# The inverses of the even mixer without zero padding: 64x64 products, two banks side by side, masks and copies on 128 partitions

## The chip, the cores and the metric

The kernel runs on one core of a Trainium2 chip. The time is device microseconds of one execution; given are the median of three runs and their range. A shorter time is better.

## The reference, cut to what matters

The program is a decoder trunk of two residual layers on 512 tokens of width 1024, in float32. The first (even) layer has an RWKV-7 mixer with 8 heads of 64 channels beside a pooling mixer, the second attention beside a state-space layer; each is followed by a layer of 32 routed experts. The change lies in the RWKV-7 recurrence alone:

```python
def step(state, inp):
    r_t, w_t, k_t, v_t, a_t, b_t = inp
    sa = jnp.einsum('bhij,bhj->bhi', state, a_t)
    state = (state * w_t[:, :, None, :] + sa[..., None] * b_t[:, :, None, :]
             + v_t[..., None] * k_t[:, :, None, :])
    return state, jnp.einsum('bhij,bhj->bhi', state, r_t)
```

The other parts of a layer are `x += Mixer(RMSNorm(x))` and `x += HierMoE(RMSNorm(x))`.

## The kernel before, in words

The recurrence is not stepped token by token. The 512 tokens are cut into 8 chunks of 64. Inside a chunk the part with `a` and `b` is a unit lower triangular 64x64 matrix, and its inverse turns the chunk into a few products; from chunk to chunk only a 64x64 state is handed on. Two heads share the 128 partitions (64 channels each), so there are four pairs of heads, `c` = 0 to 3.

For each pair the code has generators, which hand control back after every few instructions. `prep(c)` makes scaled keys and queries: `XX[H[h], h, 0]` and `[..., 1]` for head h, and `bk`, which holds `bt` and `kt`. `H` is the lower and the upper half of the partitions. `invert(c)` makes the inverses of the 8 chunks. `chain(c)` first joins them to maps (`maps`: products `pdx`, copied to `DX`, then `pgy`, added to `XX`) and then steps through the chunks (`steps`: products `pS` and `py`). `finish(c)` normalizes the result and gates it. One call of `run_all` interleaves `chain` and `finish` of one pair with `invert` of the next and `prep` of the one after it, and with products `po` of the output projection.

`invert` starts with products of `bt`, `kt` and `XX`: `pab` (the matrix transposed, and a part of the output), `paa` (the matrix, and a part of the input) and `prk`. VectorE copies them out of PSUM through constant masks (L455, L457, L469, L473, L482), and POOL adds the unit matrix (L456, L470) or applies one more mask (L474). Then five levels double the size of the inverted diagonal blocks, b = 2, 4, 8, 16, 32. A level has two halves, of four chunks each. In a half, products of `AT` and `D` go to a bank `pg`; VectorE masks them to `Gp` (L498); products of `Gp` and `DT` go to a bank `pd`, in two terms (L505, L510); VectorE copies one term to `D` (L512) and ScalarE the other to `DT` (L513), or in the last level to `DP` (L516).

All these products are written with operands of 128 rows: the operand of head h in one half of the partitions, and zeros in the other half, so that the other head's rows, which stand in the second operand, add nothing. `AT`, `Gp`, `DP` and `DX` have room for that, `[128, 8, 2, 64]` or the like, and are zeroed once; `XX` is zeroed for each pair (L379, POOL). Since head h lands in 64 of the 128 PSUM partitions, a product is one of 128 rows by 64 columns of the array, and the two heads lie beside each other. What is padded is masked and copied in two instructions of 64 partitions each, one for each head. In the profile a float32 product of PE shows as two records.

The banks of `invert` are two PSUM tiles that are taken in turn (`bank`, tag "ps").

The order of the instructions on each engine is not that of the code: the program is built with a scheduler that runs an estimate of the timeline and puts the instructions of each engine in a fixed order, which the engine then follows. Inside that order an engine waits for semaphores. After the even mixer the memory of its tiles is given to the ring of buffers into which SyncE loads the expert weights.

## Time and profile before

| | us |
|---|---|
| median of 3 runs | 1644.34 |
| lowest, highest | 1642.44, 1648.06 |
| the profiled execution | 1643.12 |
| its span, first to last instruction | 1641.4 |
| PE busy in the span | 1528.8 |
| VectorE (DVE) busy | 819.5 |
| ScalarE (ACT) busy | 447.9 |
| GpSimd (POOL) busy | 230.4 |
| HBM read | 452.91 MB |

The mean granted TensorE clock is 0.975 of full speed. The even mixer takes about the first 380 us, its inverses lie between 111 and 334 us. The profile names engines PE (TensorE's products), PEld (its weight loads), DVE, ACT, POOL and SP (SyncE). Busy times of PE are those of overlapping products whose ends are modelled, so a busy PE is not PE at its peak. An instruction is named by its line in the kernel, its operation and its tiles, output first.

### The profile page before, as it was taken

How to read it: one execution, taken by the hardware profiler on the slowest of the kernel's cores; microseconds unless marked ns; L12 is line 12 of the kernel's file. 1: busy time of each engine (PE TensorE's matmuls, PEld its weight loads, DVE VectorE, ACT ScalarE, POOL GpSimd, SP SyncE). 2: the span in 40 equal slices, each digit the busy share in tenths (PEclk: the TensorE clock that was granted, in tenths of full speed). 3: DMA queues.
4: the chain of work that ended last, by engine and by line, in shares of the span. 5: the costliest groups of instructions: out<-in, count | busy, mean ns of one | idle time of the engine just before them, and what ended most of it. 6: DMA issues, size and time to landing. Idle time of an engine off the chain costs nothing. (4 is left out here: it accounts for less than half of the span.)

```text
span 1641.4 us, 24906 instructions
## 1 busy us (share of the span) xinstructions
PE 1528.8 (93%) x9852; PEld 886.1 (54%) x9852; DVE 819.5 (50%) x1942; ACT 447.9 (27%) x1029; POOL 230.4 (14%) x268
## 2 busy tenths in 40 slices
PE   8998988999999999999998998799999999999997
PEld 6776666776444444433348775577544444433433
DVE  5577878776233333332764694764433333322323
ACT  5234434332212121111314533741021211211110
POOL 2342331200000000000211242501000000000000
PEclk9999999999999999999999999799999999999999
DMA  7210100177899999999992262209789999999996
GB/s 223 97 65 21 51 4 2 53 295 294 337 420 419 419 420 420 420 419 418 420 387 63 66 94 59 103 26 356 308 363 420 419 420 420 419 420 421 420 420 236
DMA packets 95564, 453.62 MB, mean 276 GB/s; under 512 B 12507, under 2 KB 30715, under 8 KB 49360
## 3 DMA queue, kind: packets, MB, share of 16 engines
q1 hardware_dynamic: 88144, 438.01, 67.9%
q0 software_dynamic: 5968, 13.58, 2.4%
q8 instruction: 80, 1.31, 0.3%
q10 hardware_dynamic: 1328, 0.36, 0.1%
q14 instruction: 44, 0.36, 0.1%
HBM read 452.91 MB, written 6.78 MB: 280 GB/s over the span
## 5 line engine op out<-in xcount | busy, mean ns | idle before, releaser
L1198 PE MATMUL pgu<-w,XT 128*64 128x512 f32 x1920 | 452.4, 596 | 22.3 <-DMA w<-in_moe_w_gate 19.1
L1198 PEld LDWEIGHTS pgu<-w,XT 128*64 128x64 f32 x1920 | 141.9, 137 | 312.3 <-issue 256.6
L1288 DVE TENSOR_TENSOR x<-pc,x 128x512 f32<-128x512 f32 x240 | 149.3, 682 | 163.6 <-PE pc L1198 163.6
L1198 PE MATMUL pd<-w,hTe 128*64 128x512 f32 x960 | 213.9, 598 | 0.6 <-ACT hTe L1336 0.6
L1327 DVE SCALAR_TENSOR_TENSOR hid<-hid,gs,pgu 128x512 f32<-128x512 f32 x32 | 23.9, 747 | 242.6 <-PE pgu L1198 234.9
L1095 POOL DMA_INDIRECT rows<-rows,idx x30 | 30.0, 999 | 759.6 <-DVE O L1215 590.3
L1198 PEld LDWEIGHTS pd<-w,hTe 128*64 128x64 f32 x960 | 66.6, 137 | 122.7 <-issue 112.9
L1256 ACT ACTIVATE XT<-pga,p_norm 128x128 f32<-128x128 f32 x240 | 68.3, 371 | 195.1 <-PE pga L1198 191.3
L1345 DVE TENSOR_TENSOR ylo<-pd,yhi 128x512 fp32r<-128x512 f32 (+1 forms) x68 | 44.8, 659 | 138.8 <-ACT yhi L1344 138.8
L1326 ACT ACTIVATE hid<-pgu,gs 128x512 f32<-128x512 f32 x32 | 22.0, 688 | 288.9 <-PE pgu L1198 288.9
L1198 PE MATMUL pc<-yhi,S 128*128 128x512 f32 x240 | 100.4, 418 | 0.0
L1198 PE MATMUL pc<-ylo,S 128*128 128x512 f32 x240 | 94.9, 395 | 0.0
L1344 ACT ACTIVATE yhi<-pd 128x512 fp32r<-128x512 f32 (+1 forms) x68 | 38.9, 572 | 170.9 <-PE pd L1198 153.4
L161 DVE SCALAR_TENSOR_TENSOR wlo<-w,p_norm,whi 128x512 fp32r<-128x512 f32 (+1 forms) x72 | 56.3, 813 | 44.9 <-ACT whi L160 44.9
L160 ACT ACTIVATE whi<-w,p_norm 128x512 fp32r<-128x512 f32 (+1 forms) x72 | 46.3, 692 | 77.8 <-PE pu L665 42.3
L1198 PEld LDWEIGHTS pc<-yhi,S 128*128 128x128 f32 x240 | 45.3, 189 | 34.1 <-issue 26.0
L664 PE MATMUL pu<-hhi,whi 128*128 128x512 f32 x144 | 58.6, 411 | 0.2 <-DVE u L672 0.2
L665 PE MATMUL pu<-hlo,whi 128*128 128x512 f32 x144 | 57.8, 401 | 0.0
L1884 PE MATMUL pu<-wlo,hhi 128*128 128x512 f32 x128 | 53.4, 419 | 3.4 <-DVE wlo L161 3.4
L666 PE MATMUL pu<-hhi,wlo 128*128 128x512 f32 x144 | 55.2, 402 | 0.0
L1883 PE MATMUL pu<-whi,hhi 128*128 128x512 f32 x128 | 51.0, 416 | 1.7 <-ACT us L1895 1.7
L1885 PE MATMUL pu<-whi,hlo 128*128 128x512 f32 x128 | 52.5, 416 | 0.0
(539 smaller groups left out, 2502.7 us busy)
## 6 DMA issues: line engine op xcount, KB each, us to landing
w<-in_moe_w_down SPq DMA_DIRECT2D x120, 1024.0 KB, 20.0
w<-in_moe_w_gate SPq DMA_DIRECT2D x120, 1024.0 KB, 20.0
w<-in_moe_w_up SPq DMA_DIRECT2D x120, 1024.0 KB, 20.2
w<-in_even_w_in SPq DMA_DIRECT2D x8, 1024.0 KB, 5.2
w<-in_moe_w_gate SPq DMA_DIRECT2D x16, 512.0 KB, 8.2
w<-in_moe_w_up SPq DMA_DIRECT2D x16, 512.0 KB, 9.6
w<-in_moe_w_down SPq DMA_DIRECT2D x16, 512.0 KB, 9.3
w<-in_odd_w_in SPq DMA_DIRECT2D x8, 1024.0 KB, 5.1
```

The lines of the kernel that those rows point to most:

```text
L160: nc.scalar.activation(hi[:, k, :], w[:, k, :], AF.Copy, scale=g[:, k:k + 1])
L161: nc.vector.scalar_tensor_tensor(lo[:, k, :], w[:, k, :], g[:, k:k + 1], r32(hi[:, k, :]), op0=OP.mult, op1=OP.subtract)
L664: nc.tensor.matmul(out[j], a, hhi[:, kt, :], start=kt == 0, stop=False)
L665: nc.tensor.matmul(out[j], a, hlo[:, kt, :], start=False, stop=False)
L666: nc.tensor.matmul(out[j], b, hhi[:, kt, :], start=False, stop=kt == KD - 1)
L1198: return self.K.tc.keep_in_program_order(op(*args, **kw))
L1256: nc.scalar.activation(self.XTs[j][:, k, :], p[:, i, :], AF.Copy, scale=B.gain[:, k:k + 1])
L1288: V.tensor_tensor(self.x[:, t, c], p, self.x[:, t, c], OP.add)
L1345: self.nc.vector.tensor_tensor(yl[:, c], p, r32(yh[:, c]), OP.subtract)
L1883: nc.tensor.matmul(out[j], a, whi[:, k, :], start=kt == 0, stop=False)
L1884: nc.tensor.matmul(out[j], a, wlo[:, k, :], start=False, stop=False)
L1885: nc.tensor.matmul(out[j], b, whi[:, k, :], start=False, stop=kt == KD - 1)
```

## The change

The zero padding goes, and every product of the inverse, of `pdx` and of `pgy` reads only the 64 partitions in which its head lies. A product then uses 64 rows of the array, lower or upper, and 64 columns, lower or upper (for `pgy` 128). Which head lands in which half of PSUM is chosen for each product: `same` or `other`. Where there are two terms, they are written side by side into two banks, so that one term uses the quarters of the array that the other leaves free.

The new head of `invert`, with the helper that issues the products:

```diff
+        x = lambda z: lambda h: s.XX[H[h], h, z]
+        of = lambda t: lambda h: t[H[h]]
+        across = lambda t: lambda h: t[H[1 - h]]
+        halves = [slice(4 * q, 4 * q + 4) for q in range(2)]
+        def products(n0, n1, *terms):
+            for i in range(n0, n1):
+                for p, o, left, right in terms:
+                    for h in range(2):
+                        nc.tensor.matmul(p[H[o(h)], i - n0, :], left(h)[:, i, :], right(h)[:, i, :],
+                                         start=True, stop=True)
+        p, p1 = c8(bank("pab")), c8(bank("pab"))
+        products(0, 8, (p, other, of(bt), x(0)), (p1, same, of(bt), x(0)))
+        for sl in halves:
+            V.tensor_tensor(AT[:, sl], p[:, sl], mab[:, None, 0:64].to_broadcast([128, 4, 64]), OP.mult)
+            G.tensor_tensor(AT[:, sl], AT[:, sl], m8("I64", 4), OP.add)
+            V.tensor_tensor(DT[:, sl], p1[:, sl], m8("m1T", 4), OP.mult)
+            G.tensor_tensor(DT[:, sl], DT[:, sl], m8("I64", 4), OP.add)
```

`paa` and `prk` are rewritten in the same way, with 16 + 16 products of 64 columns each: `paa` now gives `D` and the part `BR` of the output, `prk` the part `XT` and the second part of `XX`. `DT` comes from a product of its own and no longer from `AT` by a mask on POOL. In the levels:

```diff
-                p = bank("pg")[:, 0:256].rearrange("p (c n) -> p c n", c=4)
-                        nc.tensor.matmul(p[H[h], i, :], AT[:, 4 * q + i, h, :], D[:, 4 * q + i, :],
-                for h in range(2):
-                    V.tensor_tensor(Gp[H[h], sl, h, :], p[H[h]], m8(f"m{b}", 4)[H[h]], OP.mult)
+        two = [bank("pd").rearrange("p (z c n) -> p z c n", z=2, c=4) for _ in range(2)]
+            Gp = Gps[:, n % 2]
+                p = two[q][:, n % 2]
+                products(4 * q, 4 * q + 4, (p, same, across(AT), across(D)))
+                V.tensor_tensor(Gp[:, sl], p, m8(f"m{b}", 4), OP.mult)
-                p = bank("pd").rearrange("p (z c n) -> p z c n", z=2, c=4)
+                p, p1 = [t[:, (n + 1 + q) % 2] for t in two]
+                terms = [(p, same, of(Gp), of(DT))]
                 if b < 32:
-                    V.tensor_copy(D[:, sl, :], p[:, 1])
-                    A.activation(DT[:, sl, :], p[:, 0], AF.Copy)
+                    terms.append((p1, other, of(DT), of(Gp)))
+                products(4 * q, 4 * q + 4, *terms)
+                if b < 32:
+                    V.tensor_copy(D[:, sl], p1)
+                    A.activation(DT[:, sl], p, AF.Copy)
                 else:
-                    for h in range(2):
-                        A.activation(DP[H[h], sl, h, :], p[H[h], 0], AF.Copy)
+                    A.activation(DP[:, sl], p, AF.Copy)
```

`Gp` gets two buffers, for odd and even levels, and `AT` two, for odd and even pairs. In `maps`:

```diff
-                    nc.tensor.matmul(p[H[h], i, :], DP[:, 4 * q + i, h, :], s.XT[:, 4 * q + i, :],
+                    nc.tensor.matmul(p[H[h], i, :], DP[H[h], 4 * q + i, :], s.XT[H[h], 4 * q + i, :],
-            A.activation(DX[H[0], :, 0, :], p[H[0]], AF.Copy)
-            V.tensor_copy(DX[H[1], :, 1, :], p[H[1]])
+            A.activation(DX[:, q, 0:2], p[:, 0:2], AF.Copy)
+            V.tensor_copy(DX[:, q, 2:4], p[:, 2:4])
-                    nc.tensor.matmul(p[h][:, i, :], DX[:, i, h, :], s.BR[:, 4 * q + i, :],
+                    nc.tensor.matmul(p[h][:, i, :], DX[H[h], q, i, :], s.BR[H[h], 4 * q + i, :],
```

The zero fills of `AT`, `Gp`, `DP`, `DX` and `XX` go. The yields of one inverse are 24 instead of 25.

The scheduler makes a new order of it. First VectorE, in the first two halves of the first level of pair 2 (`Gp` is the mask, `Dm` the copy to `D`, `SV` and `XX` belong to the chain of pair 1). Before:

```order
L498 TENSOR_TENSOR Gp_140<-pg_2398,c_mask_107 64x4x64 x2
L498 TENSOR_TENSOR Gp_140<-pg_2444,c_mask_107 64x4x64 x2
L547 TENSOR_TENSOR XX_1465<-pgy_2560,XX_1465 128x2x256
L547 TENSOR_TENSOR XX_1465<-pgy_2561,XX_1465 128x2x256
L561 TENSOR_SCALAR SV_1600<-pS_2621,PC_1463 64x64
L438 TENSOR_TENSOR m_v2_126<-pb_2227,m_v2_126 128x512
L512 COPY Dm_2311<-pd_2462 128x256
L512 COPY Dm_2311<-pd_2481 128x256
```

and in the changed kernel:

```order
L495 TENSOR_TENSOR Gp_140<-pd_2446,c_mask_107 128x256
L478 TENSOR_TENSOR XT_2038<-prk_2380,c_mask_107 64x8x64 x2
L552 TENSOR_SCALAR SV_1617<-pS_2527,PC_1490 64x64
L529 COPY DX_1399<-pdx_2578 128x256
L495 TENSOR_TENSOR Gp_140<-pd_2447,c_mask_107 128x256
L552 TENSOR_SCALAR SV_1617<-pS_2672,PC_1490 64x64
L504 COPY Dm_2279<-pd_2447 128x256
L538 TENSOR_TENSOR XX_1492<-pgy_2624,XX_1492 128x2x256
L538 TENSOR_TENSOR XX_1492<-pgy_2625,XX_1492 128x2x256
```

Four masks of 64 partitions have become two of 128; the masks to `XT` have moved into the level; the two halves stand apart, and between the second mask and the first copy to `D` there is one `SV`.

Second PE, late in the levels of pair 1, with what each instruction waits for in brackets (the products of `AT` and `D`, then the two terms of each half). Before:

```order
L505 MATMUL pd_2144<-DT_1692,Gp_140 64x64 x7
L510 MATMUL pd_2144<-Gp_140,DT_1692 64x64 x8
L495 MATMUL pg_2185<-Dm_1691,AT_139 64x64 [waits Activation_49]
L495 MATMUL pg_2185<-Dm_1691,AT_139 64x64 x7
L495 MATMUL pg_2203<-Dm_1691,AT_139 64x64 [waits Activation_49]
L495 MATMUL pg_2203<-Dm_1691,AT_139 64x64 x7
L505 MATMUL pd_2214<-DT_1692,Gp_140 64x64 [waits DVE_49,PE_49]
L505 MATMUL pd_2214<-DT_1692,Gp_140 64x64 x7
```

and in the changed kernel (1816 and 1817 are the two banks):

```order
L451 MATMUL pd_1816<-Dm_1649,AT_139 64x64 [waits Activation_49]
L451 MATMUL pd_1816<-Dm_1649,AT_139 64x64 x7
L451 MATMUL pd_1817<-Dm_1649,AT_139 64x64 [waits DVE_49]
L451 MATMUL pd_1817<-Dm_1649,AT_139 64x64 x7
L451 MATMUL pd_1816<-DT_1650,Gp_140 64x64 [waits DVE_49]
L451 MATMUL pd_1816<-DT_1650,Gp_140 64x64 x7
L451 MATMUL pd_1817<-Gp_140,DT_1650 64x64 [waits DVE_49]
L451 MATMUL pd_1817<-Gp_140,DT_1650 64x64 x7
```

Before, the second term (L510) followed the first without a wait of its own; now it stands in the other bank and waits once more. In both kernels eight products of one term stand together.

Third PE again, between the inverses of pairs 1 and 2. Before:

```order
L535 MATMUL pdx_2281<-XT_1519,DP_145 64x128 x7
L450 MATMUL pab_2297<-XX_1872,bk_1924 64x128 [waits PE_49,Activation_49]
L450 MATMUL pab_2297<-XX_1872,bk_1924 64x128 x7
L467 MATMUL paa_2313<-bk_1924,XX_1872 64x128 [waits DVE_49,PE_49,Pool_49]
L467 MATMUL paa_2313<-bk_1924,XX_1872 64x128 x7
L543 MATMUL pgy_2328<-BR_1518,DX_1358 128x128 [waits Activation_49]
L543 MATMUL pgy_2328<-BR_1518,DX_1358 128x128 x3
L543 MATMUL pgy_2329<-BR_1518,DX_1358 128x128 [waits DVE_49]
L543 MATMUL pgy_2329<-BR_1518,DX_1358 128x128 x3
```

and in the changed kernel:

```order
L526 MATMUL pdx_2325<-XT_1550,DP_144 64x128 x8
L451 MATMUL pab_2282<-XX_1923,bk_1978 64x64 [waits DVE_49,PE_49]
L451 MATMUL pab_2282<-XX_1923,bk_1978 64x64 x15
L451 MATMUL paa_2341<-bk_1978,XX_1923 64x64 [waits Activation_49]
L451 MATMUL paa_2341<-bk_1978,XX_1923 64x64 x15
L534 MATMUL pgy_2418<-BR_1549,DX_1399 128x128 [waits Activation_49]
L534 MATMUL pgy_2419<-BR_1549,DX_1399 128x128
L451 MATMUL paa_2342<-XX_1923,bk_1978 64x64 [waits DVE_49,PE_49]
L451 MATMUL paa_2342<-XX_1923,bk_1978 64x64 x15
L451 MATMUL prk_2380<-bk_1978,XX_1923 64x64 [waits DVE_49,PE_49,Pool_49]
L451 MATMUL prk_2380<-bk_1978,XX_1923 64x64 x15
L534 MATMUL pgy_2418<-BR_1549,DX_1399 128x128
```

Eight products of 128 columns have become sixteen of 64 for each bank, and the products of `pgy` are now spread among them.

## Rows read from the trace of the kernel before

**Rows 1.** The page's totals: engine, busy us, share of the span, instructions.
```profile
PE 1528.8 (93%) x9852; PEld 886.1 (54%) x9852; DVE 819.5 (50%) x1942; ACT 447.9 (27%) x1029; POOL 230.4 (14%) x268
```

**Rows 2.** Stages: from:to, length, busy us by engine, granted clock, DMA share, GB/s.
```profile
131.00:161.50 30.50, 23.46 (x448) 17.23 (x447) 27.74 (x64) 11.88 (x22) 8.99 (x11) 0.94 0.01 2
161.50:182.90 21.40, 19.17 (x140) 13.96 (x142) 16.29 (x21) 9.35 (x17) 5.80 (x5) 1.00 0.00 1
194.30:230.50 36.20, 29.04 (x474) 21.77 (x472) 31.71 (x60) 17.29 (x34) 7.86 (x9) 0.91 0.17 60
230.50:248.60 18.10, 17.01 (x258) 15.29 (x260) 10.73 (x22) 6.54 (x17) 8.38 (x12) 1.00 0.01 2
248.60:285.70 37.10, 30.48 (x502) 22.74 (x498) 31.87 (x59) 15.84 (x33) 5.97 (x5) 0.95 0.01 2
285.70:303.90 18.20, 17.02 (x257) 15.08 (x258) 11.45 (x23) 6.46 (x16) 8.43 (x12) 1.00 0.01 2
303.90:333.90 30.00, 26.21 (x500) 21.17 (x495) 24.22 (x51) 9.96 (x24) 0.00 (x0) 1.00 0.21 72
```

**Rows 3.** The same view behind the inverses and among the experts.
```profile
328.00:369.00 41.00, 36.90 (x329) 29.31 (x330) 29.97 (x72) 13.67 (x40) 2.04 (x3) 1.00 0.76 295
451.00:492.00 41.00, 41.00 (x204) 17.04 (x201) 15.00 (x44) 8.02 (x21) 1.98 (x2) 1.00 1.01 420
```

**Rows 4.** SyncE's queue, 300 to 336 us: waiter, releaser, total us, times, longest.
```profile
SPq L1491 <- PE pd L505: 11.1, 1, 11.1
```

**Rows 5.** Waits of PE, 182 to 336 us, same columns.
```profile
PE pd L505 <- DVE Gp L498: 9.4, 12, 1.6
PE pg L495 <- ACT DT L513: 6.6, 7, 2.9
```

**Rows 6.** Groups, 111 to 336 us: shapes, count, busy us, mean ns, idle before.
```profile
L498 DVE TENSOR_TENSOR Gp<-pg,c_mask 64x256 f32<-64x256 f32 x80 | 33.7, 421 | 5.6 <-PE pg L495 4.0
...
L512 DVE COPY Dm<-pd 128x256 f32<-128x256 f32 x32 | 13.4, 421 | 5.6 <-PE pd L510 4.6 <-PE pS L559 0.5
L513 ACT ACTIVATE DT<-pd 128x256 f32<-128x256 f32 x32 | 12.2, 381 | 39.4 <-DVE Dm L512 36.2 <-DVE d L708 2.8
...
L547 DVE TENSOR_TENSOR XX<-pgy,XX 128x512 f32<-128x512 f32 x12 | 8.0, 687 | 1.0 <-PE pgy L543 0.8
...
L561 DVE TENSOR_SCALAR SV<-pS,PC 64x64 f32<-64x64 f32 x21 | 6.1, 289 | 0.8 <-ACT SV L560 0.3
...
L482 DVE TENSOR_TENSOR XX<-prk,c_mask 64x512 f32<-64x512 f32 x8 | 5.5, 689 | 4.2 <-PE prk L479 4.2
...
L538 DVE COPY DX<-pdx 64x512 f32<-64x512 f32 x6 | 4.2, 694 | 0.2 <-ACT DX L537 0.2
...
L537 ACT ACTIVATE DX<-pdx 64x512 f32<-64x512 f32 x6 | 3.5, 586 | 3.4 <-PE pdx L535 3.4
L457 DVE TENSOR_TENSOR BR<-pab,c_mask 128x256 f32<-128x256 f32 x8 | 3.4, 424 | 0.2
```

**Rows 7.** PE in order of time: start, us, line, rows*columns of the tile, records.
```profile
209.13 1.06 PE L505 MATMUL pd<-DT,Gp 128*64 128x64 f32 x16 [1.26 <-DVE Gp L498]
...
224.19 0.69 PE L505 MATMUL pd<-DT,Gp 128*64 128x64 f32 x16
...
234.96 2.05 PE L543 MATMUL pgy<-BR,DX 128*128 128x128 f32 x16
...
244.48 1.15 PE L479 MATMUL prk<-XX,bk 128*64 128x64 f32 x32
```

**Rows 8.** PE with tiles of 64 rows, one in the even, the rest in the odd mixer.
```profile
133.60 1.12 PE L337 MATMUL pz<-tw,lw 64*128 64x512 f32 x2
...
994.55 0.44 PE L2063 MATMUL pyy<-s_M,s_U 128*64 128x128 f32 x4
994.92 0.65 PE L2067 MATMUL pyy<-s_Q,s_XP 64*64 64x128 f32 x8
995.50 0.51 PE L1883 MATMUL pu<-whi,hhi 128*128 128x512 f32 x1
```

More of the change, by code (lines that the diff above doesn't have):

```diff
@@ L315, in even_mixer @@
     S = [Ctx() for _ in range(4)]
-    AT = P.tile([128, 8, 2, 64], F32, name="AT")
-    Gp = P.tile([128, 8, 2, 64], F32, name="Gp")
-    G.memset(AT, 0.0)
+    ATs = P.tile([128, 2, 8, 64], F32, name="AT")
+    Gps = P.tile([128, 2, 8, 64], F32, name="Gp")
     Y = tc.alloc_tile_pool(name="even_y", bufs=1, side="right")
-    DP = Y.tile([128, 8, 2, 64], F32, name="DP")
-    for z in (Gp, DP):
-        G.memset(z, 0.0)
+    DP = Y.tile([128, 8, 64], F32, name="DP")
     cen = P.tile([128, 128], F32, name="cen")
@@ L445, in invert @@
         bt, kt = s.bk[:, 0], s.bk[:, 1]
[L446 to L459 removed]
+        AT = ATs[:, c % 2]
@@ L460, in invert @@
+        same, other = (lambda h: h), (lambda h: 1 - h)
         s.D = Z.tile([128, 8, 64], F32, name="Dm")
         s.DT = Z.tile([128, 8, 64], F32, name="DT")
-        for q in range(2):
-            sl = slice(4 * q, 4 * q + 4)
-            p = bank("paa").rearrange("p (c n) -> p c n", c=4)
-            for i in range(4):
-                for h in range(2):
-                    nc.tensor.matmul(p[H[h], i, :], s.XX[:, h, 0, 4 * q + i, :], s.bk[:, :, 4 * q + i, :],
-                                     start=True, stop=True)
-            V.tensor_tensor(s.D[:, sl, :], p[:, :, 0:64], m8("m1", 4), OP.mult)
-            G.tensor_tensor(s.D[:, sl, :], s.D[:, sl, :], m8("I64", 4), OP.add)
-            for h in range(2):
-                o = 64 * (1 - h)
-                V.tensor_tensor(s.XT[H[h], sl, o:o + 64], p[H[h], :, 64:128], m8("low", 4)[H[h]], OP.mult)
-                G.tensor_tensor(s.DT[H[h], sl], AT[H[h], sl, h], m8("m1T", 4)[H[h]], OP.mult)
-            yield
@@ L476, in invert @@
-        p = c8(bank("prk"))
-        for i in range(8):
-            for h in range(2):
-                nc.tensor.matmul(p[H[1 - h], i, :], kt[:, i, :], s.XX[:, h, 1, i, :], start=True, stop=True)
+        D, DT = s.D, s.DT
+        p, p1 = c8(bank("pab")), c8(bank("pab"))
[5 more added lines that the diff above has]
+            G.tensor_tensor(DT[:, sl], DT[:, sl], m8("I64", 4), OP.add)
@@ new lines, in invert @@
+        yield
+        p, p1 = c8(bank("paa")), c8(bank("paa"))
+        products(0, 8, (p, other, x(0), of(bt)), (p1, same, of(bt), x(1)))
+        for sl in halves:
+            V.tensor_tensor(D[:, sl], p[:, sl], m8("m1", 4), OP.mult)
+            G.tensor_tensor(D[:, sl], D[:, sl], m8("I64", 4), OP.add)
+        V.tensor_tensor(s.BR[:, :, 64:128], p1, mab[:, None, 64:128].to_broadcast([128, 8, 64]), OP.mult)
+        yield
+        p, p1 = c8(bank("prk")), c8(bank("prk"))
+        products(0, 8, (p, same, x(0), of(kt)), (p1, other, of(kt), x(1)))
@@ L480, in invert @@
+        for h in range(2):
+            o = 64 * (1 - h)
+            V.tensor_tensor(s.XT[H[h], :, o:o + 64], p[H[h]], m8("low")[H[h]], OP.mult)
         for h in range(2):
             o = H[1 - h]
-            V.tensor_tensor(s.XX[o, h, 1], p[o], mab[o, None, 64:128].to_broadcast([64, 8, 64]), OP.mult)
+            V.tensor_tensor(s.XX[o, h, 1], p1[o], mab[o, None, 64:128].to_broadcast([64, 8, 64]), OP.mult)
+        yield
         drain(tokens(bank, kt, lambda h: s.XX[H[1 - h], h, 0]))
@@ L738, in even_mixer @@
     hp.release()
-    DX = Y.tile([128, 4, 2, 128], F32, name="DX", tag="DX")
-    G.memset(DX, 0.0)
+    DX = Y.tile([128, 2, 4, 128], F32, name="DX", tag="DX")
     CHb = tc.alloc_tile_pool(name="even_chb", bufs=2, side="right")
```

38 lines of the change are left out of this document (4 added, 34 removed).

## The prediction

> **What bounds the kernel now.** I read the totals first, then the even mixer stage by stage, then the groups of its instructions, then the waits. The totals give PE as the busiest engine [rows 1], but that is a mean over projections, mixers and experts; the change touches only the even mixer. Its chain of waits is no help, because it breaks off after the last steps of the program. So I cut the mixer into stages by the times at which the inverses of its four pairs of heads (0 to 3) begin and end [rows 2]. The reader is to see two kinds of stage there. While an inverse runs its five doubling levels (131 to 161.5, 194.3 to 230.5, 248.6 to 285.7, 303.9 to 333.9 us), VectorE is busy 27.74 of 30.50, 31.71 of 36.20, 31.87 of 37.10 and 24.22 of 30.00 us. Between two inverses (230.5 to 248.6, 285.7 to 303.9) it is PE: 17.01 of 18.10 us. In the levels PE is busy less of the time, and its waits are for the masks that VectorE writes and for the copies behind them [rows 5]: in 182 to 336 us 9.4 us for Gp and 6.6 us for DT. VectorE works through its queue in order, and the queue holds the preparation of the next pair and the end of the one before. A level takes about 7.4 us of the clock (37.1 / 5), though one mask, one copy and two groups of products take about 2.5.
>
> Whether time saved here arrives at the end is read further down the trace. SyncE's queue waits 11.1 us for the last products of the fourth inverse before it issues the expert weights, since these take over its memory [rows 4]. After that the DMA engines climb from 295 to 420 GB/s and stay full [rows 3]. Both the start of the loads and the start of the experts hang on the mixer's end, so I carry a microsecond saved before 334 us to the end as one microsecond.
>
> The profiled execution took 1643.12 us, 1.2 less than the median of 1644.34; I sum against it.
>
> **The change part by part.**
>
> 1. Masks in the levels. Before, one level needs four masks on 64 partitions, now two on 128. A 64x256 mask takes 421 ns and a 128x256 one, from PSUM by the same sort of constant, 424 [rows 6], so twice the partitions cost nothing. Five levels: 20 x 0.421 = 8.4 becomes 10 x 0.424 = 4.2, 4.2 us per pair off VectorE. This counts as far as VectorE sets the pace. For pairs 1 to 3 I take its busy shares in their levels, 0.88, 0.86, 0.81: 4.2 x 2.55 = 10.7. Pair 0 is followed by a stage that waits for the preparation of pair 1, with VectorE busy 16.29 of 21.40: I count half, 2.1. Term: -12.8, with bounds 0 (something else always late) and -16.8 (all four in full).
>
> 2. Between the inverses. VectorE per pair: before 4 AT, 2 BR, 2 D and 4 XT masks at 0.42 and two of 64x512 at 0.689, 6.4 us; now 2 AT, 2 DT, 2 D at 0.42, one 128x512 at about 0.69 and four of 64x512 at 0.689, 6.0: -0.4. PE: the 16 products of prk become 32, and at the 1.15 us that 32 records (16 products) take, of which 0.22 is the end of the last, that adds 0.9. The products for pgy took 2.05 us for 16 records of full height [rows 7]; with half the rows and two banks in turn they may run in pairs: between 0 and -0.95 each, twice per pair, and I take half, -0.9. POOL's work gets less, but it is not the one waited for here (8.4 of 18.1 us). Net -0.4 for three pairs: -1.3. Bounds: +1.5 (pgy gains nothing) and -5 (pgy gains all, and POOL's lighter work brings as much per pair as VectorE's, 0.4).
>
> 3. More changes of tile shape on PE. Before, the products of the inverse and those of the chain (pS, py) all used 128x64 tiles. Now the inverse uses 64x64 tiles, the chain stays. Counting neighbours in the order, a pair's stretch goes from 26 changes of shape to 49. What one costs, the trace shows in the odd mixer [rows 8]: records that follow each other at 55 to 57 ns are 0.20 us apart where 128*64 meets 64*64, and where 64*64 meets a full array, so 0.15 us a change. 23 x 0.15 = 3.4 us per pair on PE. In the levels PE has 4 to 7 us to spare per pair, so I charge half for three pairs: +5.2, bounds 0 and +10.4.
>    The Trainium skill says in "TensorEngine Tiling (Array Packing)", Key Properties, that a change of tiling mode, not just of tile, drains the array; the 0.15 us agree with it.
>
> 4. Two banks for everything. The two halves of a level now share two fixed banks. The order shows the waits: the second term of half 0 (into the second bank) waits for VectorE once more, behind the mask of half 1, and the first term of half 1 waits for ScalarE's copy of half 0, which read the same bank. Before, each half had its own bank and its two terms followed each other. Behind the waiting products on PE stand the chain's products; VectorE's copy of D waits for them. The cost is a group of products, 0.69 us [rows 7], and its delay of about 0.2, so up to 0.9 a level if nothing stands between. Between mask and copy the new order of VectorE mostly has two or more other instructions, 0.69 us each where they are 128x512; in one or two levels per pair it has less (in the first, one SV of 0.29 us between the second Gp and D) [rows 6]. Term: +3, bounds 0 and +13.5 (15 levels x 0.9). The inverse's end has the same: its last product waits for the copy before it. That is inside these bounds.
>    It also means that the four quarters of the array, which the two terms could fill, are seldom filled at the same time: most groups are eight products of one term, then eight of the other. So I take no faster products in the levels.
>
> 5. DX on 128 partitions: VectorE's copy from 0.694 to about 0.42 (the 128x256 copy of D), ScalarE's from 0.586 to 0.381 (that of DT) [rows 6]; with pgy, twice after the last inverse: -1.0, bounds -2.4 and 0. The zero fills that go were POOL's, beside other work: I count nothing, and if they held something up, their going is a gain inside term 2's lower bound.
>
> Sum: -12.8 - 1.3 + 5.2 + 3 - 1.0 = -6.9, 1636.2 us. Predicted: 1636 us.
>
> **The rivals.**
>
> A, larger gain. VectorE's queue is really all that counts, and changes of shape and bank waits fall into gaps. Then terms 1, 2 and 5 stand at -16.8, -1.3 and -1.0, or about 1624 us. For it: VectorE's busy shares. Against it: PE is busy 0.80 to 0.87 of the same levels.
>
> B, no change. The coupled banks hand the saved time back: term 4 at 10 instead of 3, 1643 us. For it: PE's waits for Gp and DT are already the largest ones in the stage [rows 5], and the new order puts more of them in series. Against it: VectorE always has other work to put between.
>
> C, slower: pairs of half-height products run one after the other. Each pair of products in a level (row half 1 into column half 0 and the reverse) now comes from two row halves and writes one bank. If these shared the bank in turns, 16 records would take 0.22 + 15 x 0.055 = 1.05 us, not the 0.69 of now, as they do where the clock is low (1.06 us) [rows 7]. One inverse has 640 records; 27 ns more on each is 17 us of PE per pair, against some 6 spare in the levels and 2 that the other terms free: +9 per pair in three and about half of that in the first, near 1675 us in full. It decides from 12 ns more a record on, where the 8 us are used up (about 40 ns); at 45 ns it gives about 1655. Against it: the odd mixer has such pairs, row half h into column half h of one bank, at 128 columns [rows 8]: (0.65 - 0.27) / 7 = 54 ns a record, while a single half-height product takes (1.12 - 0.64) / 1 = 0.48 us for 512 columns, 0.12 for 128. So two did run side by side. What no row shows is 64 columns and the crossed halves, where the loading of weights could set the pace.
>    The Trainium skill's rule in "TensorEngine Tiling (Array Packing)", Gotcha 1: PSUM Pressure, is that different row tiles cannot access the same PSUM bank at once. By that rule C would hold in full. The 54 ns of the odd mixer speak against it, and I let these decide.
>    The granted clock belongs to the same side: it was 0.91 and 0.95 in the levels of pairs 1 and 2 and 1.00 in those of pair 3 [rows 2], that is, part of them ran at the lower of the two levels, 1.2 GHz. If PE is idle more between its groups, there may be more of that; the difference between 36.2 and 30.0 us holds other work too, so I put at most 3 us per pair on it.
>
> **How the numbers follow.** What a measurement of this kernel can tell from no change is 0.3%, 5 us. The forecast's own case (a gain of 4 to 14 us) has 0.50, A 0.20, B 0.14, C 0.16. The forecast's case lies across the 5 us bound with little of it, 0.02. So faster 0.68, same 0.16, slower 0.16. The forecast's own range is 1629 to 1640; to hold 8 in 10 it has to take in most of A below and B and the milder part of C above: 1621 to 1650. Terms 3 and 4 at their upper bounds together, with term 1 at -8, give 1657, so the upper end is not idle.
>
> **What would show it.** Term 1: the Gp group reads 40 x about 424 ns. Term 2: the stretch from the last Gp of one inverse to the first of the next stays at 17 to 18 us. Term 3: more "issue" time ahead of PE's weight loads, about 0.15 us a change. Term 4: VectorE's copy of D waits for PE oftener than the 4.6 us that it did, but by no more than about 3 us. C: a group of 16 records of pd takes over 0.85 us at full clock. Arrival: the loads of the expert weights, which now start right behind the last stage of rows 2, at about 334 us, start some 6 us earlier, and the stages behind them keep their length. If they start much earlier and the end does not follow, my one-for-one is wrong; if they start at 340 or later, term 1 is.

## The result: slower by 0.8%, where 0.4% faster was forecast

The changed kernel takes 1658.65 us (median of 6 runs, 1653.96 to 1660.38 but for one disturbed run of 2953.44, which is left out of the ratio), the kernel before 1642.43 beside it. The ratio is 1.0078, 95% interval 1.0057 to 1.0099: 9 to 16 us slower. The forecast was 1636, and its range ended at 1650. The profiled execution took 1655.69 us with a span of 1653.9.

The totals of the changed kernel, as in [rows 1]:

```profile
PE 1535.9 (93%) x10236; PEld 886.4 (54%) x10236; DVE 793.1 (48%) x1890; ACT 441.5 (27%) x1021; POOL 205.7 (12%) x240
```

VectorE lost 26 us of work, GpSimd 25, and still the time rose. The stages, cut as in [rows 2] (four inverses and the three stretches between them; same columns, the seventh figure is the granted clock):

```profile
127.80:172.30 44.50, 34.12 (x470) 24.09 (x470) 31.94 (x63) 18.64 (x35) 7.76 (x8) 0.81 0.01 2
172.30:187.10 14.80, 14.08 (x295) 12.23 (x292) 6.92 (x15) 2.97 (x8) 4.79 (x7) 1.00 0.01 2
187.10:236.20 49.10, 38.26 (x570) 27.95 (x570) 33.37 (x59) 20.89 (x43) 7.44 (x10) 0.85 0.13 45
236.20:251.60 15.40, 14.68 (x289) 12.90 (x285) 6.83 (x14) 2.97 (x8) 4.74 (x7) 0.93 0.01 2
251.60:294.30 42.70, 35.20 (x568) 25.38 (x570) 30.85 (x55) 17.85 (x38) 7.00 (x6) 0.92 0.01 2
294.30:308.80 14.50, 13.78 (x291) 12.00 (x288) 6.88 (x14) 2.97 (x8) 4.74 (x7) 1.00 0.02 3
308.80:342.70 33.90, 30.46 (x552) 23.38 (x552) 22.78 (x47) 11.88 (x29) 0.61 (x1) 1.00 0.19 64
```

The levels became longer, 44.5, 49.1, 42.7 and 33.9 us against 30.5, 36.2, 37.1 and 30.0, and the stretches between them shorter, 14.8, 15.4 and 14.5 against 32.8 (161.5 to 194.3, of which rows 2 shows the first part), 18.1 and 18.2. Part of that is only moved: the order now puts more of the chain and of the next pair's preparation between the levels. The end tells what is left. The last level ends 8.8 us later (342.7 for 333.9), SyncE, which waits for it, starts the weight loads 9.8 us later (344.60 for 334.77), and the span is 12.5 us longer. Behind the inverses the stages are as they were, answering [rows 3] and [rows 4]:

```profile
337.80:378.80 41.00, 37.13 (x362) 29.41 (x359) 26.45 (x67) 12.42 (x39) 2.04 (x3) 1.00 0.76 296
461.00:502.00 41.00, 41.00 (x212) 18.25 (x213) 16.85 (x46) 9.60 (x25) 1.98 (x2) 1.00 1.01 419
```

```profile
SPq L1481 <- PE pd L451: 14.8, 1, 14.8
```

So most of the time is lost in the inverses. Two things changed there. The first is who waits. Groups of the changed kernel, 111 to 345 us (the second term on PE, the mask of the first product, the copy of D, the copy of DT), answering [rows 6]:

```profile
L451 PE MATMUL pd<-Gp,DT 64*64 64x64 f32 x512 | 24.4, 242 | 12.0 <-DVE Gp L495 7.2 <-DVE Dm L504 4.7
L495 DVE TENSOR_TENSOR Gp<-pd,c_mask 128x256 f32<-128x256 f32 x40 | 16.5, 418 | 8.7 <-PE pd L451 8.4
L504 DVE COPY Dm<-pd 128x256 f32<-128x256 f32 x32 | 13.4, 420 | 10.7 <-PE pd L451 10.6
L505 ACT ACTIVATE DT<-pd 128x256 f32<-128x256 f32 x32 | 12.1, 378 | 49.0 <-PE pd L451 48.9
```

Before, the second term never waited (the same view of the kernel before):

```profile
L510 PE MATMUL pd<-Gp,DT 128*64 128x64 f32 x512 | 23.6, 234 | 0.0
```

PE's waits from 187 to 345 us, answering [rows 5]:

```profile
PE pd L451 <- DVE Gp L495: 11.2, 12, 3.0
PE pd L451 <- DVE Dm L504: 5.5, 6, 3.8
PE pd L451 <- ACT DT L505: 4.5, 9, 1.1
```

The wait for D is new; it and the one for Gp fall in part on the second term. Before, that term stood right behind the first term of its half. Now it waits 12.0 us in all, for the mask of the other half and for the copy of D, because it writes a bank which those still read. One level on PE's timeline shows the chain that results, in the order first term and second term of half 0, first term of half 1, second term of half 1 (its first two records):

```profile
229.45 0.68 PE L451 MATMUL pd<-DT,Gp 64*64 64x64 f32 x16 [2.17 <-DVE Gp L495]
230.38 0.68 PE L451 MATMUL pd<-Gp,DT 64*64 64x64 f32 x16 [0.25 <-DVE Gp L495]
231.54 0.80 PE L451 MATMUL pd<-DT,Gp 64*64 64x64 f32 x10 [0.48 <-ACT DT L505]
232.04 0.37 PE L451 MATMUL pd<-Gp,DT 64*64 64x64 f32 x2
```

The second thing is the clock. All stretches within the inverses in which the granted clock was 0.50, that is 1.2 GHz, summed: six in the changed kernel, then four in the kernel before (length, busy time by engine):

```profile
sum 40.96, PE 32.44 PEld 24.76 DVE 21.67 ACT 9.75 POOL 4.14; mean PE 5.41 PEld 4.13 DVE 3.61 ACT 1.63 POOL 0.69
```

```profile
sum 13.65, PE 13.01 PEld 11.22 DVE 12.41 ACT 3.21 POOL 4.12; mean PE 3.25 PEld 2.81 DVE 3.10 ACT 0.80 POOL 1.03
```

PE worked 32.44 us at half the clock, where it had been 13.01. At full clock this work would take no less than half as long, so the low clock cost PE at most 16.2 us against 6.5. (A group of 16 records took 1.12 us at the low clock, at 281.22 us, and 0.68 at the full one, so for such groups it was less.) From the first mask to the last copy of DP, the two kernels compare like this (before, then changed):

```profile
132.30:336.00 203.70, 174.21 (x2736) 137.22 (x2732) 162.94 (x315) 84.37 (x177) 54.01 (x68) 0.97 0.07 23
```

```profile
129.80:345.00 215.20, 180.38 (x3028) 138.49 (x3029) 137.95 (x261) 76.97 (x169) 36.96 (x45) 0.90 0.06 21
```

Of the 11.5 us more, PE is idle for 5.3 (34.8 for 29.5) and busy for 6.2. The low clock accounts for at most 9.7 us more of PE's time; without that much, its work would have shrunk by 3.5. What PE did ahead of a fall, here of the one at 279.35 us:

```profile
275.50:279.30 3.80, 1.38 (x48) 1.10 (x48) 3.77 (x4) 0.38 (x1) 2.95 (x2) 1.00 0.00 0
```

It waited for 2.4 of 3.8 us, while VectorE worked through four long instructions. So this idle time on PE was paid twice, once by itself and once by the clock behind it.

### The profile page after: what moved, and what is told of

Same layout as the page of the kernel before. It is cut to its first block, busy times and chain, and to the rows that moved or that the text cites. A ratio compares the mean times of both kernels' runs of the same rounds, so it can differ in the third digit from the quotient of the medians.

```text
span 1653.9 us, 25543 instructions
## 1 busy us (share of the span) xinstructions
PE 1535.9 (93%) x10236; PEld 886.4 (54%) x10236; DVE 793.1 (48%) x1890; ACT 441.5 (27%) x1021; POOL 205.7 (12%) x240
```

## The experiments

Seventeen kernels, each with the kernel before on the same chip (its medians: 1646.20 us beside e1 to e4, 1644.98 beside e5 to e8, 1643.71 beside e9 to e12, 1644.89 beside e13 to e15, 1640.94 beside e16 and e17). The last column is the ratio to before, with its 95% interval; 0.001 is 1.64 us. e11, a small program of its own that was run once (630.70 us), is not in the table. Only e13 to e16 hold an order; in all the others the scheduler made a new one.

| run | what it is | median us | ratio to before |
|---|---|---|---|
| e1 | changed, banks of its own per half | 1646.68 | 1.0014 (0.9994 to 1.0034) |
| e2 | changed, straight products | 1671.88 | 1.0175 (1.0147 to 1.0204) |
| e3 | before, with the shared banks | 1667.60 | 1.0154 (1.0122 to 1.0187) |
| e4 | changed, first pair earlier | 1654.59 | 1.0066 (1.0040 to 1.0092) |
| e5 | e1 with split masks | 1656.15 | 1.0064 (1.0048 to 1.0079) |
| e6 | before, 64x64 products in the levels | 1664.52 | 1.0112 (1.0095 to 1.0130) |
| e7 | e1, terms in a third set of banks | 1660.03 | 1.0083 (1.0070 to 1.0096) |
| e8 | changed, second term in a third bank | 1658.63 | 1.0065 (1.0043 to 1.0086) |
| e9 | e6 with a rule of order | 1663.68 | 1.0119 (1.0097 to 1.0141) |
| e10 | before, whole masks by padding DT | 1645.57 | 1.0010 (0.9997 to 1.0022) |
| e12 | e1 with the rule of order | 1644.92 | 1.0003 (0.9989 to 1.0017) |
| e13 | e6 in the order of before | 1650.33 | 1.0036 (1.0021 to 1.0051) |
| e14 | before in the order of e6 | 1657.04 | 1.0075 (1.0057 to 1.0092) |
| e15 | e10, PE in the order of before | 1646.73 | 1.0001 (0.9987 to 1.0014) |
| e16 | e5 in the order of e1 | 1667.14 | 1.0138 (1.0111 to 1.0165) |
| e17 | changed, with the rule of order | 1659.25 | 1.0094 (1.0074 to 1.0114) |

### The shared banks: e1, e2, e3

e1 gives each half its own bank again. I kept products that cross (row half 0 into column half 1) out of a bank that straight ones of the other row half write; no run tries the two together. So e1 also makes all products straight (those of `pab` and `paa` too, not shown), and its code writes the two terms one after the other instead of in turn:

```
-two = [bank("pd")... for _ in range(2)]
-    p = two[q][:, n % 2];  products(..., (p, same, across(AT), across(D)))
+    p = bank("pg")[:, 0:256]...;  products(..., (p, same, of(AT), of(D)))
-    p, p1 = [t[:, (n + 1 + q) % 2] for t in two]
+    t = bank("pd")...;  p, p1 = t[:, 0], t[:, 1]
```

> The changed kernel, but in the levels each half of the chunks has a bank of its own again for its first product and one for its two terms, as before the change, and all products of the inverse go straight (row half h into column half h), since crossed ones could not share a bank. Masks and copies stay on 128 partitions, products stay 64x64. Theory of the shared banks: the waits of PE for Gp and of VectorE for pd in the levels go back from 18.0 and 19.0 us to about 12 and 9, the low-clock stretches of the four inverses go back from 41 to about 14 us, and the time is 1642 or less, down to 1634. Rival, the order of the first pair (its levels stand behind the first output products, which they still do here): 1650 to 1657. Rival, 64x64 products as such (shape changes, less of the array in use): 1650 or more.

e2 has the straight products alone, on the shared banks (`pab` and `paa` again not shown):

```
-products(4 * q, 4 * q + 4, (p, same, across(AT), across(D)))
+products(4 * q, 4 * q + 4, (p, same, of(AT), of(D)))
-    terms.append((p1, other, of(DT), of(Gp)))
+    terms.append((p1, same, of(DT), of(Gp)))
```

> The changed kernel with the two shared banks kept, only that all products of the inverse go straight (row half h into column half h) where some were crossed; this is the step between the changed kernel and the one with banks of its own. Theory of the shared banks: no difference to the changed kernel, 1652 to 1661. Rival, crossed quadrants cost something (the loads of weights, the clock): it is faster by 5 us or more, 1650 or less.

e3 puts the shared banks into the kernel before:

```
-    p = bank("pg")[:, 0:256]...
+    p = two[q][:, n % 2]
-    p = bank("pd")...
+    p, p1 = [t[:, (n + 1 + q) % 2] for t in two]
```

> The kernel before with one part of the change alone: in the levels the first product and the two terms of both halves use the same two banks, side by side, as the changed kernel does; products stay full height with zero padding, masks on 64 partitions. Theory of the shared banks: slower by 6 to 14 us than before, 1648 to 1656, with more waits of PE for Gp and of VectorE for pd. Rivals (order of the first pair, 64x64 products): 1640 to 1646, as before, unless the order moves too.

The shared banks, with the order that the scheduler makes for them, make the kernel before 25 us slower (e3: 20 to 31), and taking them out of e2, which else differs from e1 only in how its code writes the two terms, gives back 26 (1.0175 less 1.0014). In the changed kernel they cost less, 10 us (1.0078 less 1.0014) to 12 (less e12's 1.0003), or 6 to 16 with the intervals of these runs. No run holds the order while it takes the banks apart. But the shared banks are slower than those of e1 in every order that was run: changed 1.0078, e4 1.0066 and e17 1.0094 against e1 1.0014 and e12 1.0003.

Why they cost less in the changed kernel, no run separates. There the crossed second term can use the quarters of the array that the first leaves idle: where the two ran in turn, at 275.50 us, their 32 records took 0.70 us, hardly more than the 16 of one term (0.68). e2, which can't do that, is 16 us behind the changed kernel; but its order is another one too. That was in none of my expectations: for e2 I had no difference, or a faster kernel. The second term on PE and the copy of D in e1, and then the second term in e3, 111 to 356 us:

```profile
L451 PE MATMUL pd<-Gp,DT 64*64 64x64 f32 x512 | 22.9, 225 | 0.0
L502 DVE COPY Dm<-pd 128x256 f32<-128x256 f32 x32 | 13.3, 419 | 10.7 <-PE pd L451 10.6
```

```profile
L511 PE MATMUL pd<-Gp,DT 128*64 128x64 f32 x512 | 23.9, 240 | 7.4 <-DVE Gp L499 5.0 <-DVE Dm L513 2.3
```

With the banks apart the second term's wait is gone, and with the banks shared it is there, whatever the products' height. In e1 the copy of D still waits 10.6 us for PE, as in the changed kernel; I had expected 9 for copy and masks together, so that wait is not the banks'. From the first mask to the last copy of DP, e1:

```profile
134.50:337.80 203.30, 176.38 (x3026) 137.15 (x3027) 136.45 (x261) 77.01 (x169) 37.30 (x45) 0.95 0.07 23
```

It is as long as in the kernel before (203.70), and most of the clock comes back with the banks. Its stretches at the low level, summed, against 40.96 us with PE busy for 32.44 in the changed kernel (I had expected about 14 of them):

```profile
sum 20.49, PE 16.41 PEld 12.46 DVE 11.81 ACT 7.36 POOL 2.68; mean PE 5.47 PEld 4.15 DVE 3.94 ACT 2.45 POOL 0.89
```

So e1's 1646.68 lies between my theory (1642 or less) and its rivals (1650 or more): taking the banks apart removes the loss and leaves no gain. e3's 1667.60 lies above all that I had expected for it.

### Other layouts of banks: e7, e8

```
 e7 (on e1):       -t = bank("pd")...       +t = acc("pd")...
 e8 (on changed):  +p = bank("pg")...;  p, p1 = bank("pd")..., acc("pd")...
```

> The version with banks of its own for each half, and the two terms of a level in a third set of banks (those that the chain and the output products take in turns), so that the first product of the next level does not wait until both copies have read the bank. If waits between the halves and levels are the price, this goes on where the version with own banks stopped: PE's wait for DT (4.6 us there) goes and the time is 1634 to 1642. Rival, those banks are wanted by the chain, which then waits for the levels: 1647 or more.

> The changed kernel with its crossed products, but the first product and first term of each half have rotating banks as before the change, and the second term a bank of its own from those of the chain: four quarters of the array can work at once, and no bank is shared by the halves. The step from straight to crossed products was worth 13 us with shared banks. If that holds here as well, it beats before: 1630 to 1640. Rival, crossing only helped because the halves were coupled: 1642 to 1650, like the version with own banks.

Both failed. e7 comes out where its rival had it, but not by the rival's waits: PE's wait for DT is gone (4.6 us in e1), the chain's products hardly wait, and PE waits for other work of VectorE instead. The two longest, 134.4 to 344 us:

```profile
PE ptk L399 <- DVE bk L391: 8.3, 2, 5.4
PE pp L700 <- DVE d L697: 7.5, 3, 3.9
```

In e8, too, no two halves share a bank, and it is slower than both its theory and its rival. Why these two layouts lose stays open; each has an order of its own. e8 from its first mask to its last copy of DP:

```profile
133.20:343.00 209.80, 172.13 (x3018) 129.36 (x3018) 134.26 (x252) 74.71 (x166) 39.25 (x47) 0.88 0.05 19
```

PE is busy less than in any other run, 172.13 us, although a clock of 0.88 means that about 50 of the 209.80 us were at the low level (2 x 0.12 x 209.8). But 37.7 us are idle, and the low clock takes part of the saved work back.

### Half height, or the order: e6, e9, e13, e14, e11

e6 is the kernel before with only the height of its level products changed:

```
-matmul(p[H[h], i, :], AT[:, 4 * q + i, h, :], D[:, 4 * q + i, :], ...)
+matmul(p[H[h], i, :], AT[H[h], 4 * q + i, h, :], D[H[h], 4 * q + i, :], ...)   # and both terms alike
```

> The kernel before, with one part alone: the three products of a level take only the 64 rows of their own half, so that they are 64x64 and not 128x64 with zeros; tiles, masks, copies and banks stay as before. By term 3 of the prediction (each change of shape 0.15 us, half of it charged): 1646 to 1656. Rival, the change of shape falls into gaps: 1640 to 1646. Rival, products of half height let the clock fall oftener: more low-clock time than the 14 us of before within the inverses, and 1650 or more.

It was 18 us slower, three times term 3. Its third rival had both the time and the low clock right (43 us of it within the inverses). But the order had moved too: the scheduler reckons 64x64 products otherwise, and the output products of the first stage slipped ahead of the first pair's last level. e9 holds these back by a rule, and e13 and e14 hold everything: a table of the order that the scheduler gave to the one kernel is laid on the other, instruction by instruction.

```
 e9:   -run_all((first, ...), (prep(1), 10), (part(pool_out, 2), 2))
       +run_all((first, ...), (prep(1), 10))
       +drain(issued_after(tc, S[0].last, part(pool_out, 2)))      # S[0].last: last product of pair 0
 e13:  e6 + order of every even-mixer instruction on PE, VectorE, ScalarE, GpSimd as in before
 e14:  before + the order of e6
```

> The kernel before with 64x64 products in the levels, as in the run that was 18 us slower; new is one rule of order alone: the first output products on PE are issued behind the last products of the first pair's inverse, as they stand in the kernel before (there the 64x64 form had let them slip ahead of the last level). Theory of the order: the time goes back to 1641 to 1648 and the low-clock time within the inverses to 14 to 20 us. Rival, products of half height hold the clock less well and change shape oftener: low-clock time stays at 30 us or more and the time at 1655 to 1666.

> The kernel before with 64x64 products in the levels, and every instruction of the even mixer on TensorE, VectorE, ScalarE and GpSimd held in exactly the order of the kernel before. Only the height of 1792 products differs. Theory of the order (half height costs nothing by itself; the scheduler's new order let TensorE's idle time gather and the clock fall): 1640 to 1648, low-clock time within the inverses 10 to 20 us. Rival, half height itself (clock, changes of shape): 1655 or more with 30 us or more at the low clock. Half and half: 1648 to 1655.

> The reverse: the kernel before, full-height products, with every instruction of the even mixer held in the order that the scheduler gave the version with 64x64 products. No instruction differs from the kernel before, only the order. Theory of the order: 1655 to 1666, as that version, with 30 us or more of low clock within the inverses. Rival, half height itself: 1641 to 1648.

The rule did nothing (e9: 1.0119, where e6 had 1.0112). The full orders settle it for e6: half height costs 6 us (e13: 3 to 8) and the order that the scheduler makes of it 12 (e14: 9 to 15), with not one instruction changed; together the 18 of e6. From the first mask to the last copy of DP, e13 and e14:

```profile
129.90:338.80 208.90, 181.10 (x2735) 140.68 (x2730) 163.21 (x314) 84.17 (x177) 53.98 (x68) 0.95 0.07 22
```

```profile
129.50:347.10 217.60, 180.87 (x2735) 142.11 (x2731) 164.84 (x314) 83.38 (x177) 54.73 (x68) 0.93 0.07 21
```

In e13 PE is idle for 27.8 us, no more than before, and busy for 6.9 more; in e14 idle for 36.7, and the clock is lower. Part of e13's 6.9 is the clock, too. Its stretches at the low level, summed, against 13.65 us with PE busy for 13.01 before:

```profile
sum 20.48, PE 19.29 PEld 14.56 DVE 15.04 ACT 7.39 POOL 3.38; mean PE 3.86 PEld 2.91 DVE 3.01 ACT 1.48 POOL 0.68
```

That is at most 3.1 us of the 6.9 (half of 6.3). By time, 1650.33 us, e13 lies in the range that I had set for half and half. e11 measures the height by itself, with nothing but groups of products that wait for a copy of the group before:

> The disputed cost by itself; all of the model is left out and the output is only the input. Nine stages, each after 24 dense products of 128x512: 30 groups of small products with 64 columns into one bank, each group waiting for VectorE's copy of 128x256 of the group before. Forms: full height with zeros (128x64), half height straight (64x64, row half h into column half h), half height crossed (64x64 in four quarters, two banks). Groups of 8 products and one copy, 16 and one, 8 and two. If half height holds the clock less well: at the same group time and copy time the granted clock is 1.0 in the full-height stage and well below in the half-height stage of the same size (0.5 to 0.9). Rival, the clock only follows idle time: the same clock, within 0.05, in the full and the straight stage of a size. A group of 8 takes 0.69 us at full clock in the first two forms, and less in the crossed one.

Its stages: full, straight and crossed, first 8 products to a copy, then 16:

```profile
31.00:78.00 47.00, 31.70 (x481) 26.46 (x480) 12.32 (x29) 0.00 (x0) 0.00 (x0) 0.55 0.01 2
100.00:145.90 45.90, 30.60 (x482) 25.34 (x481) 12.32 (x29) 0.00 (x0) 0.00 (x0) 0.58 0.01 1
168.00:202.80 34.80, 20.40 (x482) 15.08 (x481) 12.32 (x29) 8.03 (x29) 0.00 (x0) 0.56 0.01 1
225.50:275.30 49.80, 34.51 (x962) 30.43 (x961) 12.30 (x29) 0.00 (x0) 0.00 (x0) 1.00 0.01 2
296.10:345.70 49.60, 34.32 (x961) 30.27 (x961) 12.30 (x29) 0.00 (x0) 0.00 (x0) 1.00 0.01 2
366.50:403.00 36.50, 34.38 (x962) 30.36 (x961) 12.73 (x30) 11.11 (x29) 0.00 (x0) 1.00 0.02 4
```

Full and half height are alike in time and in clock (0.55 and 0.58; 1.00 and 1.00; with 8 products and two copies 0.54 and 0.54). The rival was right here: in these stages the clock does not mind the height. That leaves e13's 6 us to the changes of shape, which e11 does not have, and to the clock behind them; this is an inference, since no run measures the changes alone.

### The order in the changed kernel: e4, e12, e17

```
 e4:        -N0, N1, N2, N3 = 18, 5, 24, 6     +N0, N1, N2, N3 = 20, 5, 24, 6
 e12, e17:  the rule of e9     (on e1; on changed)
```

> The changed kernel with two more steps of the first pair's preparation and inverse laid beside the projection (20 for 18), so that more of its levels stand ahead of the first output products and of the preparation of pair 1. Theory of the shared banks: little changes, 1652 to 1660. Rival, the order of the first pair: since 11 of the 12 us arose there, at least 5 come back, 1652 or less.

> The version with banks of its own for each half (64x64 products, whole masks), with the rule that the first output products on PE are issued behind the first pair's last level. Theory of the order: the masks' 9 us come out at last, 1633 to 1641. Rival, half height and the clock: no better than without the rule, 1643 to 1650.

> The changed kernel with one rule of order: the first output products on TensorE are issued behind the last products of the first pair's inverse, as in the kernel before. If the loss of the first pair (11 of 12 us at its end) comes from those products standing ahead of its last levels: 1644 to 1651. Rival, the waits of the shared banks make it, and the order is only where they show: 1652 to 1662.

11 us of the delay stood at the end of the first pair (its last copy of DP ends at 174.3 us, before at 163.1), and I took the output products ahead of its last levels for the cause. Neither moving the levels up (1.0066) nor holding those products back (1.0094) changed anything beyond the intervals, and with own banks there was nothing to win by it (1.0003 after 1.0014). So the place of these products was not the cause of the loss.

### What whole masks are worth: e5, e16, e10, e15

```
 e5 (on e1):  -V.tensor_tensor(Gp[:, sl], p, mask)
              +for h in range(2): V.tensor_tensor(Gp[H[h], sl], p[H[h]], mask[H[h]])
 e16:         e5 + the order of e1, the two parts of a mask side by side
 e10:         before, Gp in one mask, DT padded in place of Gp (ScalarE: two copies of 64x256 for one)
 e15:         e10 + PE in the order of before
```

> The version with banks of its own for each half, but the masks Gp again by 64 partitions: 80 of 0.42 us for 40, so VectorE gets back the 16.8 us that term 1 of the prediction counted. If VectorE sets the pace of the levels, as term 1 had it: 9 to 17 us slower than the version with whole masks, 1655 to 1663. Rival, the masks' time lay beside waits for PE and ScalarE and was worth little: 0 to 4 us, 1646 to 1651.

> The version with banks of its own for each half, masks again by 64 partitions (80 of 0.42 us for 40), and every other instruction of the even mixer held in the order of that version with whole masks; the second half of a mask stands right behind the first. It prices the masks with the order held, where the first split (9.5 us slower) let the scheduler choose anew. If VectorE sets the pace, as term 1 of the prediction had it: 8 to 17 us slower than with whole masks, 1653 to 1663. Rival, most of that was the order: 0 to 5 us, 1645 to 1651.

> The kernel before with whole masks alone: the zero padding moves from Gp to DT, so VectorE writes Gp by 40 masks of 128x256 in place of 80 of 64x256, and ScalarE copies DT by 64 partitions, twice as many copies. Products stay full height, banks and setup stay as before, no part of the array changes shape. If the masks are worth what the split of them cost in the version with own banks (9.5 us): 1633 to 1639. Rival, ScalarE's second copy of DT (0.38 us on the way to the next level, 10 per pair less the last) takes it back: 1641 to 1646.

> The version with whole masks through padding of DT (which came out at the time of before), with TensorE's instructions of the even mixer held in the order of the kernel before; the other engines are ordered by the scheduler. If the order ate the masks' gain: 1632 to 1640. Rival, ScalarE's second copy or something else on the chain eats it: 1641 to 1650.

Splitting the masks again costs 8 us where the scheduler may choose anew (e5 against e1), and 20 in e1's own order, which is not made for it (e16, above its expected range). Term 1's 12.8 lies between; neither run holds an order that suits both forms. Yet e10 and e15, with the same 40 masks fewer at full height, gained nothing. In their trace the names Gp and DT of these two tiles are swapped. The two products on PE that wait in a level, before, and in e15 with the copies on ScalarE:

```profile
L505 PE MATMUL pd<-DT,Gp 128*64 128x64 f32 x640 | 29.1, 234 | 12.1 <-DVE Gp L498 11.9
L495 PE MATMUL pg<-Dm,AT 128*64 128x64 f32 x640 | 28.4, 233 | 11.1 <-ACT DT L513 11.0
```

```profile
L505 PE MATMUL pd<-Gp,DT 128*64 128x64 f32 x640 | 29.7, 238 | 3.7 <-DVE DT L498 3.5
L496 PE MATMUL pg<-Dm,AT 128*64 128x64 f32 x640 | 28.8, 235 | 15.4 <-ACT Gp L514 12.3 <-DVE Dm L512 1.8 <-DVE DT L498 1.3
L514 ACT ACTIVATE Gp<-pd 64x256 f32<-64x256 f32 x64 | 24.1, 376 | 30.2 <-DVE Dm L512 27.3 <-DVE dtmp L708 2.2
```

PE's wait for the masks falls from 12.1 to 3.7 us, so the whole masks do arrive sooner; but there are twice the copies, and the product behind them waits 15.4 us where it waited 11.1. The second copy stands in the chain from level to level, where the mask's second half had stood. This I read from the trace, and it accounts for half of what the masks gave; no run has the masks whole and the copies single at full height. Nor does a run beat before: e1, e10, e12 and e15 are level with it.

## Why the prediction was wrong, point by point

**Term 4, shared banks: +3, measured +10 to 12 (e1 and e12 against the changed kernel). This is the step that failed, as far as the runs single one out.** The waits were the ones that the order showed, but I priced them as groups of products with other work between, level by level, and the profile of before can't show how often that work is there. The second term, which never waited, waits 12.0 us on PE, and 0.0 in e1. The sign that I had named, VectorE's copy of D, read 10.6 us where I had allowed about 3 more than 4.6; but e1 reads 10.6 as well, so it does not measure the banks. Rival B, which had the banks at 10, had both mechanism and size, but ended at no change because it left the rest of the sum as it was.

**The rest of the sum: -9.9, measured +2.3 (e1) or +0.5 (e12).** The forecast missed by about 20 us, from -6.9 to +12.8. Term 4 makes up 7 to 9 of them. The other 10 to 12 are a gain that did not come: without the shared banks the changed kernel only draws level with the kernel before. Which of terms 1, 2, 3 and 5 lost it, or whether a new order did, stays open; what the runs show of each follows.

**The order had no term.** The scheduler ranks the instructions by its own reckoning, and in these runs new durations or banks gave a new order. In the kernel before such a new order alone cost 12 us (e14), as much as the largest term of my sum. I had counted its changes of shape, but read its waits only at three places. How much it cost the changed kernel itself stays open: its instructions are not those of before, so that order could not be laid on it.

**The clock stood outside the sum.** I put at most 3 us per pair on it, under rival C alone. It took up to 9.7 us more of PE's time in the inverses, behind stretches in which PE waited. e11 shows that height does not bring it, and in e1, without the second term's wait, at most 1.7 us of it are left (16.41 less 13.01, halved).

**Term 3, changes of shape: +5.2, measured at most +6 (e13: 3 to 8, with the clock in it).** The size is right with the order held, though no run changes the shapes alone. What I said would show it didn't: "issue" time ahead of the levels' weight loads fell from 14.5 us (the first two rows, before) to 6.7 (the third), and in e13 it is 13.3.

```profile
PEld pd L505 <- issue: 11.9, 12, 1.7
PEld pg L495 <- issue: 2.6, 4, 0.8
PEld pd L451 <- issue: 6.7, 11, 1.5
```

**Term 1, masks: -12.8; undoing it costs 8 to 20** (e5, e16), and doing it alone gains nothing (e10, e15). The group reads 40 x 418 ns for the 424 of the forecast. The masks take less of VectorE, as forecast; as a gain over the kernel before no run shows them.

**Terms 2 and 5** were not measured alone. Of their parts, prk takes 4.1 us more in all four pairs, 1.0 each, as forecast; pgy takes 2.1 us less in three pairs, 0.7 each for the 0.9 of the forecast; the copies of DX take 424 and 373 ns. The stretch from the last mask of one inverse to the first of the next, which was to stay at 17 to 18 us, is 14.8, 15.6 and 14.7: work of it has moved into the levels.

**One for one held**, nearly: the loads start 9.8 us later and the span is 12.5 us longer. The rest may be the clock: 0.89 at 392 to 440 us, where the matching 383 to 431 us of before had 1.00. By the sign that I had named, loads that start at 340 us or later, term 1 was to be wrong; they start at 344.60, but a late start tells no term from another.

**Rival C** ends in the right place for the wrong reason: its decider, a group of 16 records above 0.85 us at full clock, did not come (0.68 us), and e11 finds half-height products no slower. **Rival A** fell with term 4.

So with the terms as measured, masks (-8 to -20) and shape (+6 at most) should leave e1 with a gain of 2 us or more, and e1 shows none (1.0014, 0.9994 to 1.0034). The difference is terms 2 and 5 and the order, which e1 does not take apart, or masks that are worth less than their splitting costs.

## What to carry to other kernels

Before a change shares a buffer between two streams, count the waits that it adds between them, and price each at the whole delay until the other stream's reader has run, not at the group of work that is late; take the share out (as e1 did), or put it in alone (as e3 did), before judging the rest of the change. Where a scheduler sets the order, give the order its own uncertainty, and test an edit with the order held; here an order alone was worth 12 us. And on TensorE look for the clock behind idle time, which here cost a second time. Not all idle time does that: in e11's straight stage of 16 products PE was idle for 15.3 of 49.6 us, and the clock stayed at 1.00.

## What the runs showed that I had not expected

Four quarters of the array do run at once. In e11 the first turn of 16 products takes 1.15 us straight and 0.69 crossed into two banks, and a group of the changed kernel with both terms in turn takes as long as the latter (the three in this order; x33 counts one dense product that was ending):

```profile
296.02:297.17 1.15, 1.15 (x33) 1.01 (x32) 0.00 (x0) 0.00 (x0) 0.00 (x0) 1.00 0.00 0
366.47:367.16 0.69, 0.69 (x33) 0.56 (x32) 0.00 (x0) 0.00 (x0) 0.00 (x0) 1.00 0.00 0
275.50:276.20 0.70, 0.69 (x32) 0.56 (x32) 0.67 (x2) 0.00 (x0) 0.00 (x0) 1.00 0.00 0
```

In e11's later turns the gain, 1.22 us for 1.65 with the copy (36.5 and 49.6 us for 30 turns), comes another way: VectorE's copy waits for the first bank's 8 products only and runs beside those of the second (in the turn from 367.68 us the copy starts at 368.41, and the second bank's products end at 368.74). And less work on PE did not keep its clock up: e8 has the least PE work of the runs and a clock of 0.88 in the inverses, with PE idle for 37.7 us.
